# Low parts of 36 weight chunks: negated on ScalarE and completed by an accumulating DMA, in place of a VectorE subtraction

## The chip, the cores and the metric

The kernel runs on one core of a Trainium2 chip. The metric is the device time of one execution in microseconds (us), lower being better. Five engines work side by side, each with its own queue of instructions that it takes in order: TensorE (PE in the profile; PEld is its loading of weights), VectorE (DVE), ScalarE (ACT), GpSimd (POOL) and SyncE (SP). They wait for each other, and for the DMA transfers that they issue, by semaphores.

## The reference

The kernel computes a decoder trunk of two layers, in float32, for 256 tokens of width 2048:

```python
for i in range(DEPTH):                       # DEPTH = 2
    u = rmsnorm(h, mix_pre_g[i])
    if i < N_A:                              # layer 0
        m = short_conv_mixer(u, a_w_in[i], a_conv_w[i], a_w_out[i])
    else:                                    # layer 1
        m = stick_breaking_mixer(u, b_w_q[j], k_sh, v_sh, b_w_o[j])
    h = h + rmsnorm(m, mix_post_g[i])
    u = rmsnorm(h, mlp_pre_g[i])
    h = h + rmsnorm(square(relu(u @ mlp_w_up[i])) @ mlp_w_down[i], mlp_post_g[i])
    if i == N_A - 1:
        k_sh, v_sh = split(rmsnorm(h, kv_norm_g) @ w_kv)
```

`w_in` is 2048 x 6144, the other mixer matrices are 2048 x 2048 or 2048 x 4096, and the MLP's hidden width is 8192.

## The kernel before, in words

**High and low parts.** A matmul takes operands rounded to a shorter format (float32r). To keep the precision, each operand is split into a high part, its rounded value, and a low part, the rest: `hi = round(w)`, `lo = w - hi`. A product is then three matmuls, high by high, high by low and low by high. So every weight that comes in has to be split.

**The stream of weights.** All weights come as one list, `stream`, of 768 chunks of 128 x 1024 float32 (512 KB). `load_one` has SyncE load the next chunk into one of `RAW` = 5 buffers `raw`. `split_one` splits the next chunk: `high_parts` has ScalarE write `hi` (line 173) and `low_part` has VectorE write `lo` (line 184; line 186 where a gain is multiplied in). Both go into rings of `RING` = 7 buffers. After a split the raw buffer is given back and the next load is traced; the load waits until all who read the buffer are done. SyncE takes its loads in order, so those behind a waiting load wait too. `chunk(i)` is called where TensorE uses chunk i, and splits up to `AHEAD` = 4 chunks further.

**Sevens.** Some pairs of chunks, those in the dictionary `sevens`, are used in a scheme with seven products in place of eight. `split_seven` makes four differences of the two raw chunks on VectorE (line 210, the tile `sums`), and splits them and the chunks into four buffers of each ring (named a, b, t and u).

**Input projection.** After a lead, tiles of two chunks and seven pairs alternate. A tile takes the 8 high matmuls of its first chunk, the 8 of its second, and then the low ones in the same order (line 748). The outcome is evicted by `combined` (line 757, the tile `sum`).

**MLP.** The hidden width is cut into `STEPS` = 8 steps. In each of the first seven, two halves (h = 0 and 1) have four up tiles each, and after every up tile one pair of down chunks for the step before (a seven, or an eight). An up tile (`whole_up`) takes two chunks: 16 high matmuls (line 1013), then 16 low ones (line 1020). All these up tiles use one PSUM bank: ScalarE copies half of it (`half`, line 1026), VectorE adds the other half to that (`s`, line 966), and only then can the next up tile begin. Within a step the chunks lie 16 to a half and 4 to an up tile with its pair, so 16h + 4 and 16h + 5 are the chunks of the second up tile of half h, and 16h + 10 and 16h + 11 the pair after the third.

**Accumulating DMAs.** `add_later` evicts four PSUM banks of products to SBUF once in a step (twice in the first), and eight or nine DMAs from GpSimd's queue, issued in `finish` (line 1030), add these 256 KB tiles to the partial results in SBUF (`mg`, by `accum_op=ALU.add`).

**Order.** TensorE's order is that of the program. The other engines' orders come from a planner that runs at build time, with its own estimates of times; within the norms the orders of VectorE and ScalarE are written out by hand.

Of the kernel before, what the change touches and what calls it, by code (L numbers as in the profile page):

```python
# [9 lines left out]
F32 = mybir.dt.float32  # L10
F32R = mybir.dt.float32r
AF = mybir.ActivationFunctionType
ALU = mybir.AluOpType
# [5 lines left out]
KD = D // P  # L19
# [27 lines left out]
STEPS = 8  # L47
# [20 lines left out]
IN_AT = {unit: KD * LEAD // CH + 2 * i for i, unit in enumerate(IN_UNITS)}  # L68
# [27 lines left out]
def trunk(ctx, tc, x, xT, vecs, rows, ws, out):  # L96
    nc = tc.nc
# [45 lines left out]
    raw, parts, early = {}, {}, {}  # L143
    last_load = [None]
    count = {"loaded": 0, "split": 0, "limit": 1 << 30, "apart": False}
    lows = []
    sevens = {}

    def load_one():
        i = count["loaded"]  # L150
        if i >= len(stream):
            return
        w, c = stream[i]
        t = wpool.tile([P, CW], F32, tag="raw", name=f"raw{i}")
        n = HALF if i < FIRST else CW
        for a in range(0, CW, n):
            last_load[0] = nc.sync.dma_start(t[:, a : a + n], w.ap[c, :, a : a + n])
        raw[i] = t
        count["loaded"] += 1

    def pieces_of(i):
        w, c = stream[i]
        gains = w.gains(c) if w.gains else [None] * (4 if i < FIRST else 1)
        n = CW // len(gains)
        return [(slice(j * n, (j + 1) * n), gain) for j, gain in enumerate(gains)]

    def high_parts(i):
        while count["loaded"] <= i:
            load_one()
        hi = wsplit.tile([P, CW], F32R, tag="hi", name=f"whi{i}")  # L170
        lo = wsplit.tile([P, CW], F32R, tag="lo", name=f"wlo{i}")
        for j, (at, gain) in enumerate(pieces_of(i)):
            rounded = nc.scalar.activation(  # L173
                hi[:, at], raw[i][:, at], AF.Copy, scale=1.0 if gain is None else gain
            )
            if j < 2:
                early[i] = rounded
            if not count["apart"]:
                low_part(hi, lo, raw[i], at, gain)
        parts[i] = hi, lo  # L180

    def low_part(hi, lo, t, at, gain):
        if gain is None:
            nc.vector.tensor_tensor(lo[:, at], t[:, at], hi[:, at].bitcast(F32), op=ALU.subtract)  # L184
        else:
            nc.vector.scalar_tensor_tensor(  # L186
                lo[:, at], t[:, at], gain, hi[:, at].bitcast(F32), op0=ALU.mult, op1=ALU.subtract
            )
# [37 lines left out]
    def split_one():  # L226
        i = count["split"]
        if i in sevens:
            split_seven(i)
            return  # L230
        high_parts(i)
        count["split"] += 1
        if count["apart"]:
            lows.append(i)
        else:
            raw.pop(i)
            load_one()
# [138 lines left out]
    h = [None] * NB  # L376
# [310 lines left out]
    W = {"in": Weights(ws["in"]), "out": Weights(ws["out"])}  # L687
# [18 lines left out]
    def convolution(tmp):  # L706
# [71 lines left out]
        scale = {}  # L778
# [104 lines left out]

        for i in range(0, KD, 2):
            sevens[IN_AT["pair", i]] = sevens[IN_AT["pair", i + 1]] = tmp
        new, late, gates = [], {}, {}
        for kind, i in IN_UNITS:
            if kind == "pair":
# [5 lines left out]
            at, n = IN_AT["tile", i], IN_TILES[i]  # L894
# [28 lines left out]
    with tc.tile_pool(name="p_in", bufs=1, reuse_waits="tile") as tmp:  # L923
        y = convolution(tmp)
# [14 lines left out]
    def mlp(pool, i, before, after):  # L939
# [3 lines left out]
        scale = [None] * NB  # L943
# [89 lines left out]
        def lead_up(to):  # L1033
            first = W["mlp", i, 0].base
            place = {kn: m for m, kn in enumerate(UP_FIRST)}
            lead = list(range(LEAD_UP))
            alone = [(k, n) for k in range(ALONE) for n in lead]
            for b in range(NB):
                for k, n in sorted(alone, key=lambda kn: (kn[0] // 4, kn[1] // 3 if kn[0] < 4 else 0)):
                    high(first, place[k, n], k, n, n + 2, b)  # L1040
            for k, n in alone:
                low(first, place[k, n], k, n)
            for k in range(ALONE, KD):
                for n in lead:
                    high(first, place[k, n], k, n, n + 2)
                for n in lead:
                    low(first, place[k, n], k, n)
                    if k == KD - 1:
                        finish(to, n)
            for n in range(LEAD_UP, NF):  # L1050
                whole_up(to, n, first + 2 * n, (n + 2) % 8)
# [114 lines left out]
        for e in range(STEPS):  # L1166
            for h in range(2):
                for m in SEVEN[e][h]:
                    n = 16 * h + 4 * ORDER[h].index(m) + 2 if e < STEPS - 1 else 8 * h + 2 * m
                    sevens[W["mlp", i, e + 1].base + n] = pool  # L1170
        now = Hidden(0)
        lead_up(now)
        for e in range(STEPS):
# [33 lines left out]
    run(project(W["out"], y, 2, sublayer(mix0)), leave=mix0)  # L1207
    kv = KeyNorms(pool0, None)
    mlp(pool0, 0, mix0, kv)


# [181 lines left out]

    pool1, mix1 = held["pool1"], held["mix1"]
    mlp(pool1, 1, mix1, OutNorms(pool1, None))
    pool1.release()

# [79 lines left out]
```

## Time and profile before

| | us |
|---|---|
| runs (three) | 2110.68, 2110.22, 2110.02 |
| median | 2110.22 |
| profiled execution, its own time | 2110.45 |
| its span, first to last instruction | 2108.7 |

| engine | busy us | share |
|---|---|---|
| TensorE | 2090.4 | 99% |
| VectorE | 1835.2 | 87% |
| ScalarE | 1435.2 | 68% |
| GpSimd | 113.7 | 5% |

The granted clock of TensorE was 0.999 of full speed. In the lines shown further on, a group's row has the line, the engine, the operation, the tiles written and read, their shapes, the count, the busy time, the mean of one in ns, and after the second bar the idle time of the engine just before them with what ended it. A wait's row names who waited for what, the total, how often, and the longest. A row of the timeline begins with the start and the length, both in us, and may end with the idle time before it in brackets. The input projection runs from the start to about 270 us, the first MLP from about 365 to 1010 and the second from about 1440 to the end.

### The profile page before, as it was taken

Reading aid. Unit: us, or ns where it says so; the run is one execution under the profiler, and the core shown is the slowest. Engines: PE = TensorE matmul, PEld = TensorE weight load, DVE = VectorE, ACT = ScalarE, POOL = GpSimd, SP = SyncE. Lnnn points to the kernel's source line nnn. Section 1 sums busy time; section 2 is a strip of 40 time slices with the busy share of each in tenths; the row PEclk is TensorE's granted clock in tenths of the full one; section 3 lists DMA queues with packets and bytes.
Section 4 is the critical chain, followed back from the end, with each engine's and each line's share of the span. In section 5 each row is a group of like instructions: output and inputs, shape, how many; then the busy total and the mean of one; then the engine's idle time right before and its main releaser. Section 6 shows DMA issues by size and latency. Waiting matters only on the chain.

```text
span 2108.7 us, 29835 instructions
## 1 busy us (share of the span) xinstructions
PE 2090.4 (99%) x10608; PEld 1782.2 (85%) x10608; DVE 1835.2 (87%) x2807; ACT 1435.2 (68%) x2210; POOL 113.7 (5%) x137
## 2 busy tenths in 40 slices
PE   9999999999999999999999999999999999999998
PEld 8888888888888888888888888889888888888886
DVE  9999965999899999999866777558989999999997
ACT  8656544776776776767567888547767767677674
POOL 0000000010110110101000000000101001011010
PEclk9999999999999999999999999999999999999999
DMA  8467574586777867868575555655778688687683
GB/s 290 155 205 250 191 259 142 190 244 213 232 230 223 265 194 236 250 205 268 173 222 165 160 160 166 218 175 170 199 237 238 213 239 242 210 255 215 220 267 137
DMA packets 132342, 449.23 MB, mean 213 GB/s; under 512 B 14816, under 2 KB 15072, under 8 KB 131168
## 3 DMA queue, kind: packets, MB, share of 16 engines
q1 hardware_dynamic: 113184, 406.55, 58.7%
q0 software_dynamic: 18720, 40.38, 9.9%
q8 instruction: 83, 1.36, 0.3%
q14 instruction: 67, 0.55, 0.1%
q10 hardware_dynamic: 288, 0.39, 0.1%
HBM read 413.19 MB, written 2.10 MB: 197 GB/s over the span
## 4 chain that ended last, share of the span: by engine, by line
PE 91%; DVE 6%; DMA 2%; issue 1%; ACT 1%; DVEq 0%; ACTq 0%
PE up L1013 20%; PE up L1020 11%; PE acc L326 8%; PE acc L328 8%; PE acc L327 8%; PE acc L748 5%; PE more L1121 4%; PE more L1120 4%; PE more L1122 4%; PE acc L1120 4%; PE acc L1121 4%; PE acc L1122 4%; PE lead L748 2%; DVE wlo L184 1%; DMA raw<-w_mlp 1%; PE up L1015 1%
## 5 line engine op out<-in xcount | busy, mean ns | idle before, releaser
L184 DVE TENSOR_TENSOR wlo<-raw,whi 128x1024 fp32r<-128x1024 f32 (+1 forms) x442 | 528.1, 1206 | 87.0 <-ACT whi L173 86.6
L173 ACT ACTIVATE whi<-raw 128x1024 fp32r<-128x1024 f32 (+1 forms) x442 | 453.0, 1043 | 171.1 <-PE acc L328 82.5
L1013 PE MATMUL up<-u,whi 128*128 128x512 f32 x1952 | 465.6, 390 | 3.5 <-DVE s L966 3.5
L1013 PEld LDWEIGHTS up<-u,whi 128*128 128x128 f32 x1952 | 364.6, 188 | 79.9 <-DVE s L966 5.4
L1020 PEld LDWEIGHTS up<-u,wlo 128*128 128x128 f32 x2048 | 263.6, 191 | 10.3
L1020 PE MATMUL up<-u,wlo 128*128 128x256 f32 x2048 | 268.0, 283 | 0.0
L1030 POOL DMA_DIRECT2D mg<-more x108 | 101.7, 1051 | 1280.5 <-ACT s L968 648.3
L186 DVE SCALAR_TENSOR_TENSOR wlo<-raw,gv,whi 128x512 fp32r<-128x512 f32 (+1 forms) x160 | 131.9, 854 | 41.5 <-ACT whi L173 40.8
L210 DVE TENSOR_TENSOR sums<-raw,sums 128x512 f32<-128x512 f32 x236 | 162.1, 687 | 1.3
L173 ACT ACTIVATE whi<-raw,gv 128x512 fp32r<-128x512 f32 (+1 forms) x160 | 121.6, 800 | 48.5 <-PE acc L328 41.8
L326 PE MATMUL acc<-whi,u 128*128 128x512 f32 x384 | 153.1, 399 | 0.1
L328 PE MATMUL acc<-whi,u 128*128 128x512 f32 x384 | 150.0, 391 | 0.0
L327 PE MATMUL acc<-wlo,u 128*128 128x512 f32 x384 | 149.8, 390 | 0.0
L1026 ACT ACTIVATE half<-up 128x256 f32<-128x256 f32 x128 | 48.5, 381 | 89.1 <-PE up L1020 85.5
L748 PE MATMUL acc<-u,whi 128*128 128x512 f32 x416 | 98.9, 391 | 2.7 <-DVE sum L757 2.7
L210 DVE TENSOR_TENSOR sums<-raw,raw 128x512 f32<-128x512 f32 x118 | 81.0, 687 | 23.2 <-DMA raw<-w_mlp 23.0
L967 ACT ACTIVATE s<-s 128x256 f32<-128x256 f32 x128 | 52.4, 413 | 66.3 <-DVE s L966 65.9
L748 PEld LDWEIGHTS acc<-u,whi 128*128 128x128 f32 x416 | 77.4, 188 | 20.5 <-DVE sum L757 3.7
L210 DVE TENSOR_TENSOR sums<-raw 128x512 f32<-128x512 f32 x118 | 81.0, 686 | 11.9 <-DMA raw<-w_mlp 11.7
L328 PEld LDWEIGHTS acc<-whi,u 128*128 128x128 f32 x384 | 72.1, 188 | 15.6
L326 PEld LDWEIGHTS acc<-whi,u 128*128 128x128 f32 x384 | 72.2, 188 | 13.8 <-ACT tk L1309 0.6
L327 PEld LDWEIGHTS acc<-wlo,u 128*128 128x128 f32 x384 | 72.3, 188 | 13.4
(5995 smaller groups left out, 4513.4 us busy)
## 6 DMA issues: line engine op xcount, KB each, us to landing
raw<-w_mlp SPq DMA_DIRECT2D x512, 512.0 KB, 4.6
raw<-w_in SPq DMA_DIRECT2D x94, 512.0 KB, 4.4
mg<-more POOLq DMA_DIRECT2D x108, 256.0 KB, 8.3
raw<-w_out SPq DMA_DIRECT2D x32, 512.0 KB, 4.5
raw<-w_v SPq DMA_DIRECT2D x32, 512.0 KB, 4.3
raw<-w_k SPq DMA_DIRECT2D x32, 512.0 KB, 4.4
raw<-w_q SPq DMA_DIRECT2D x32, 512.0 KB, 4.2
raw<-w_wo SPq DMA_DIRECT2D x32, 512.0 KB, 3.7
```

The costliest lines, as they stand in the source:

```text
L173: rounded = nc.scalar.activation(hi[:, at], raw[i][:, at], AF.Copy, scale=1.0 if gain is None else gain)
L184: nc.vector.tensor_tensor(lo[:, at], t[:, at], hi[:, at].bitcast(F32), op=ALU.subtract)
L210: nc.vector.tensor_tensor(t, x, y, op=ALU.subtract)
L326: nc.tensor.matmul(ps[:], xh, hi[:, a], start=i == 0 and k == 0, stop=False)
L327: nc.tensor.matmul(ps[:], xh, lo[:, a], start=False, stop=False)
L328: nc.tensor.matmul(ps[:], xl, hi[:, a], start=False, stop=i == self.n - 1 and k == self.ks - 1)
L748: nc.tensor.matmul(ps[:, :cols], w, xs[:, :cols], start=k == 0 and part == parts[0], stop=k == KD - 1 and part == parts[1], skip_group_che ...
L1013: nc.tensor.matmul(ps, weight(0, first, m), x, start=k == 0, stop=False)
L1020: nc.tensor.matmul(pss[n][:, :T], weight(1, first, m), x, start=False, stop=k == KD - 1)
L1120: nc.tensor.matmul(self.ps[key][:], xh, hi, start=first, stop=False)
L1121: nc.tensor.matmul(self.ps[key][:], xh, lo, start=False, stop=False)
L1122: nc.tensor.matmul(self.ps[key][:], xl, hi, start=False, stop=last)
```

## The change

For 36 chunks, collected in the set `subtracted`, VectorE's subtraction is left out. ScalarE writes `hi` as before and then, in a second pass over the raw chunk, its negative, rounded in the same way, into the `lo` buffer. A DMA from GpSimd's queue then adds the whole raw chunk (512 KB, from SBUF to SBUF) onto it, which gives `w - hi`. Eight of the 36 are the second chunks of every other tile of the input projection (tiles 5 to 19); 28 are the second chunk of the second up tile of each half, in the first seven steps of both MLPs. The raw buffer of such a chunk is read until the DMA has landed.

```diff
@@ -145,6 +145,7 @@
     sevens = {}
+    subtracted = set()
 
@@ -175,7 +176,10 @@
             if j < 2:
                 early[i] = rounded
-            if not count["apart"]:
+            if i in subtracted:
+                nc.scalar.activation(lo[:, at], raw[i][:, at], AF.Copy, scale=-1.0)
+                nc.gpsimd.dma_start(lo[:, at].bitcast(F32), raw[i][:, at], accum_op=ALU.add)
+            elif not count["apart"]:
                 low_part(hi, lo, raw[i], at, gain)
@@ -883,6 +887,7 @@
             sevens[IN_AT["pair", i]] = sevens[IN_AT["pair", i + 1]] = tmp
+        subtracted.update(IN_AT["tile", i] + 1 for i in range(5, KD + 4, 2))
@@ -1168,6 +1173,8 @@
                     sevens[W["mlp", i, e + 1].base + n] = pool
+                if e < STEPS - 1:
+                    subtracted.add(W["mlp", i, e + 1].base + 16 * h + 5)
```

## The prediction

> **What bounds the kernel now.** I read the page first: busy times and the chain that ended last.
>
> ```profile
> span 2108.7 us, 29835 instructions
> PE 2090.4 (99%) x10608; PEld 1782.2 (85%) x10608; DVE 1835.2 (87%) x2807; ACT 1435.2 (68%) x2210; POOL 113.7 (5%) x137
> ...
> PE 91%; DVE 6%; DMA 2%; issue 1%; ACT 1%; DVEq 0%; ACTq 0%
> ```
>
> TensorE carries 91% of the chain and is busy 2090.4 of 2108.7 us; VectorE, at 87%, is the next engine. So an edit that adds no TensorE work can win only what TensorE loses by waiting, and can lose without such a limit. The waits, over the whole span:
>
> ```profile
> PE acc L748 <- DVE sum L757: 4.7, 5, 1.9
> PE up L1013 <- DVE s L966: 3.5, 4, 1.8
> ...
> DVE sums L210 <- DMA raw<-w_mlp: 34.7, 27, 2.7
> ```
>
> TensorE waits 8.2 us for VectorE in all, in nine places. The third row matters as much: VectorE itself waits 27 times for a weight load in the MLPs. VectorE runs in order, so whatever stands behind such a wait waits too.
>
> Next, four stretches by engine and DMA: the input projection where its eight moved chunks lie, the steady part of the first MLP, a 27 us stretch of it in which GpSimd's accumulating DMAs run (`mg<-more`), and one of 25 us without them.
>
> ```profile
> core 0: us, PE busy (x) PEld busy (x) DVE busy (x) ACT busy (x) POOL busy (x), PEclk, DMA share, GB/s
> 76.00:230.00 154.00, 151.99 (x772) 128.86 (x770) 153.59 (x219) 94.20 (x119) 1.23 (x2) 1.00 0.67 218
> 613.00:1000.00 387.00, 387.00 (x1976) 331.64 (x1976) 366.78 (x531) 275.86 (x416) 40.12 (x46) 1.00 0.79 237
> 613.00:640.00 27.00, 27.00 (x136) 22.98 (x136) 24.84 (x41) 20.29 (x33) 7.92 (x9) 1.00 1.05 279
> 655.00:680.00 25.00, 25.00 (x126) 21.30 (x126) 22.31 (x35) 16.95 (x27) 0.00 (x0) 1.00 0.65 221
> ```
>
> From 613 to 1000 TensorE has no idle time at all: relief of VectorE there is worth nothing. In 613:640 the DMA engines are full (1.05), in 655:680 they are not (0.65). Each MLP step has one such full stretch, early in its second half (h = 1), and one moved chunk of each step (16h + 5 with h = 1) falls into it: 14 of the 36. The other 22 (14 with h = 0, eight in the input projection) meet no `mg<-more`.
>
> **The change, part by part.** Removed is one VectorE subtraction a chunk, added one ScalarE pass.
>
> ```profile
> L184 DVE TENSOR_TENSOR wlo<-raw,whi 128x1024 fp32r<-128x1024 f32 (+1 forms) x442 | 528.1, 1206 | 87.0 <-ACT whi L173 86.6
> L173 ACT ACTIVATE whi<-raw 128x1024 fp32r<-128x1024 f32 (+1 forms) x442 | 453.0, 1043 | 171.1 <-PE acc L328 82.5
> ```
>
> VectorE loses 36 x 1.21 = 43 us of 1835, ScalarE gains 36 x 1.04 = 38 us of 1435. ScalarE is 71% busy in 613:1000 (275.86 of 387), so its pass costs nothing by itself; behind it wait the high part of the next pair and the PSUM eviction `half`, for about 1 us.
>
> Added to GpSimd's queue is one accumulating DMA of 512 KB a chunk. Its price has no row in this trace; the nearest are the 256 KB accumulates and the 512 KB loads, here in 613:640:
>
> ```profile
> q1 hardware_dynamic: 1407, 5.15, 54.3%
> q0 software_dynamic: 1296, 2.36, 50.2%
> ...
> raw<-w_mlp SPq DMA_DIRECT2D x9, 512.0 KB, 6.7
> mg<-more POOLq DMA_DIRECT2D x8, 256.0 KB, 8.6
> ```
>
> GpSimd's nine instructions there (the x9 of the table above) are all accumulates of 256 KB: 50.2% of 27 us, 13.6 us of all 16 engines, 1.5 us each; twice the bytes make 3.0 us. The loads took 54.3%, 14.7 us for 5.15 MB: 1.5 us for one of 512 KB (0.524 MB). So the added transfer takes the engines 1.5 us if it goes like a load, 3.0 us like an accumulate. I take 3.0, the same operation. The Trainium skill (DMA: Bandwidth & Descriptors, "Anatomy of one DMA — SWDGE (gpsimd) path") prices a DMA from GpSimd at about 2.0 us fixed plus its bytes over 436 GB/s, which by its formula is an estimate of 1.2 us of movement for 512 KB; it makes no difference for accumulation, and the row above (1.5 us for 256 KB, where the formula has 0.6) speaks against it. By 1.2 us the sum below would come to +2.9 us instead of +22.5.
>
> *Where there is room.* Over the trace the `mg<-more` landed 3.3 us after issue at the least (row below, with the tightest of the 22 places, the first moved chunk, 27). Alone, the new one should land some 1.5 us later than that, so about 5 us after issue, 6 with loads beside it.
>
> ```profile
> DMA to landing us min/median/max: 3.3/8.3/12.3
> 75.09 1.99 ACT L173 ACTIVATE whi<-raw 128x1024 fp32r<-128x1024 f32 x2
> 77.36 2.35 DVE L184 TENSOR_TENSOR wlo<-raw,whi 128x1024 fp32r<-128x1024 f32 x2
> 84.44 1.83 PE L748 MATMUL acc<-u,wlo 128*128 128x256 f32 x14
> ```
>
> The high part ends at 77.1. Negation 1.0 and DMA 6 give 84.1; the chunk is the second half of its tile, so its low part is needed eight matmuls after 84.44, at 85.4. It fits by 1.3 us. Its raw buffer comes free some 4.5 us later than at 79.7, and with it the load five chunks on; that load has the five-deep ring as cover. I cost these 22 at nothing. If the cover is gone, it is about 1 us a place, up to 20 us. What they can win is in the input projection, where VectorE is busy 153.59 of 154 us:
>
> ```profile
> PE acc L748 <- DVE sum L757: 2.0, 3, 0.9
> ```
>
> That is the waits of 76:230 alone: at most 2.0 us, all of which I take.
>
> *Where there is none.* Around the moved chunk of 613:640 (its high part is made at 618.92), the timelines of GpSimd, ScalarE, VectorE, SyncE and TensorE:
>
> ```profile
> 613.81 0.87 POOL L1030 DMA_DIRECT2D mg<-more  x1 [67.66 <-ACT s L968]
> 617.00 0.87 POOL L1030 DMA_DIRECT2D mg<-more  x1 [2.32 <-ACT more L1082]
> 617.58 1.19 POOL L1030 DMA_DIRECT2D more<-more  x1
> 618.11 2.45 POOL L1030 DMA_DIRECT2D mg<-more  x2
> 621.57 0.87 POOL L1030 DMA_DIRECT2D mg<-more  x1 [1.00 <-DMA mg<-more]
> 626.43 0.87 POOL L1030 DMA_DIRECT2D mg<-more  x1 [3.99 <-DMA mg<-more]
> 618.92 1.06 ACT L173 ACTIVATE whi<-raw 128x1024 fp32r<-128x1024 f32 x1
> 620.39 1.23 DVE L184 TENSOR_TENSOR wlo<-raw,whi 128x1024 fp32r<-128x1024 f32 x1
> 621.64 3.10 SPq L157 DMA_DIRECT2D raw<-w_mlp  x2
> 629.82 0.69 DVE L210 TENSOR_TENSOR sums<-raw 128x512 f32<-128x512 f32 x1
> 632.67 0.69 DVE L210 TENSOR_TENSOR sums<-raw,raw 128x512 f32<-128x512 f32 x1 [2.16 <-DMA raw<-w_mlp]
> 634.41 0.42 DVE L966 TENSOR_TENSOR s<-up,half 128x256 f32<-128x256 f32 x1
> 629.51 2.08 PE L1020 MATMUL up<-u,wlo 128*128 128x256 f32 x16
> 636.21 1.07 PE L1013 MATMUL up<-u,whi 128*128 128x512 f32 x4
> ```
>
> Today the raw buffer is free at 621.6, and SyncE issues the load that waited for it, and 3 us later the next (a `seven` pair needs both). VectorE waits 2.16 us for the second, until 632.67; `s` stands behind that and empties the one PSUM bank of the up tiles at 634.83; TensorE wants it at 636.21. The slack is 1.38 us. After the change the buffer is free only when the accumulate has landed. The negation writes the buffer that VectorE could write from 620.39 on, so it ends near 620.39 + 1.04 = 621.4. By then five accumulates are in the queue, 7.5 us of engine time at 1.5 each; with four of them queued from 617.00 on, some 3 us of that is left. The new one goes behind them: 621.4 + 3 + 3.0, and up to 1.5 us of a load beside it, is 627.4 to 629. The low part is wanted at 630.5, eight matmuls into the row of 629.51, so that just fits. The load is what comes late: it is issued at about 628 instead of 621.6, and SyncE's later loads stand behind it. But the DMA engines are full, so 3.0 us more work ahead of the pair's second load moves its landing by about 3.0 us, and with it the `sums` and `s`. TensorE then stalls for 3.0 less the slack. (The 6 us of later issue don't count in full: a load that starts then meets fewer accumulates.) VectorE's 1.2 us of relief ahead of it only lengthens its wait.
>
> The same reading in all 14 places (slack = next up matmul less the end of `s`) gives, first MLP 0.09, 0.05, 1.38, 2.20, 1.50, 2.80, 1.02, second 0.46, 0.05, 1.12, 2.20, 0.89, 2.78, 1.00 us. First and last of the 14:
>
> ```profile
> 466.91 0.42 DVE L966 TENSOR_TENSOR s<-up,half 128x256 f32<-128x256 f32 x1
> 467.42 0.93 PE L1013 MATMUL up<-u,whi 128*128 128x512 f32 x3
> ...
> 2035.19 0.42 DVE L966 TENSOR_TENSOR s<-up,half 128x256 f32<-128x256 f32 x1
> 2036.61 1.07 PE L1013 MATMUL up<-u,whi 128*128 128x512 f32 x4
> ```
>
> The sum of (3.0 less slack), none below nothing, is 24.5 us. With the 2.0 us won: +22.5. The profiled execution took 2110.45 us (1.75 outside its span), 0.23 above the median of 2110.22, so the sums are made from 2110.45: **2133 us**. With 2.0 us of delay (the engines are not quite full at each instant) the 14 give 12.4 and the total is 2121; with 4.0, 38.5 and 2147.
>
> **The rivals.**
>
> *VectorE's relief wins (faster).* Mechanism: the planner orders VectorE anew, and where it puts `s` ahead of the two `sums`, the load's delay is off TensorE's path. It decides at one point: `s` before `sums<-raw,raw` in the 14 places. Then the 2.0 us of the projection and the 3.5 us of `up <- DVE s` go: 2110.45 - 5.5 = 2105 us. For it: VectorE is busy all the time in the projection and 95% of 613:1000, so it is late often. Against: in 613:640 the planner put `sums` first although it had to wait. Chance 0.27, most of it beyond 0.2%.
>
> *The accumulate queues behind more.* If its place in GpSimd's order is behind the add of 621.57, 1.5 us more stand ahead of it: 4.5 us of delay, 14 x 4.5 - 17.5 = 45.5, total 2153 us. Behind the add of 626.43, which itself waits 3.99 us for a landing, it is some 6.5 us: +71.5, 2182 us, and the low part too comes after 630.5. For it: GpSimd is in order and these adds are ready early. Against: by the estimate above the negation ends just before 621.57. Chance 0.18.
>
> *The transfer is cheaper or covered.* At a load's 1.5 us the 14 places cost 7.4, total 2116 us; with a cover I don't see, nothing, and 2108. Middle 2112. The share of 1.05 speaks against it. Chance 0.10. The Trainium skill's formula (DMA: Bandwidth & Descriptors, the section above) would end here, at 2113; no row of this trace goes by it.
>
> **How the numbers follow.** Forecast 0.45, queue 0.18, relief 0.27, cheaper 0.10. About 0.2% (4.2 us) is what a measurement of this kernel can tell from no change. Faster by more: 0.23, from the relief. Within: 0.11, the rest of the relief and most of "cheaper". Slower by more: 0.66. Range: the forecast alone is 2121 to 2147; with the relief's 2105 and the nearer queue case, 2104 to 2153 us. Left out are the second queue case and a relief above all waits I can see.
>
> **What would show it.** Right: the VectorE row of the low parts counts 406 instead of 442; the wait `sums <- DMA raw<-w_mlp` grows from 34.7 us by 20 to 40; `up L1013 <- DVE s` grows from 3.5 to about 25, in the h = 1 stretches; 655:680 and its like stay without waits. Wrong: TensorE waits for the new DMA itself at L1020 (queue rival); `s` stands ahead of `sums` and `up <- s` falls (relief); new accumulates land within 4 us in the full stretches (cheaper); waits appear in the 22 quiet places, which I costed at nothing.

## The result, and the profile after

The changed kernel takes 2232.4 us (median; 2230.7 to 2234.0), the kernel before 2110.1 beside it: a ratio of 1.058 (95% interval 1.0562 to 1.0599). It is slower by 122 us, where 22.5 were forecast. First the page of the changed kernel, with the rows that answer to those shown of before.

```profile
span 2229.3 us, 29885 instructions
PE 2123.6 (95%) x10608; PEld 1808.9 (81%) x10608; DVE 1806.3 (81%) x2771; ACT 1474.9 (66%) x2246; POOL 144.3 (6%) x173
...
PE 65%; DMA 14%; DVE 9%; issue 6%; ACT 4%; POOL 1%; POOLq 0%; DVEq 0%; ACTq 0%; SPq 0%
...
L188 DVE TENSOR_TENSOR wlo<-raw,whi 128x1024 fp32r<-128x1024 f32 (+1 forms) x406 | 485.9, 1205 | 106.1 <-ACT whi L174 91.5
```

VectorE's row of low parts lost 42 us (528.1 to 485.9) and ScalarE gained 40, as worked out; all of VectorE's busy time fell by 29 only, and what took the rest back is not shown. TensorE fell from 91% of the chain to 65%, and DMAs rose from 2% to 14%. The 120.6 us that the span grew can be split by TensorE's own row: its idle time grew from 18.3 to 105.7 us (+87.4), and its busy time from 2090.4 to 2123.6 (+33.2) with the same 10608 matmuls. TensorE's waits in the changed kernel, and who waited for loads on VectorE:

```profile
PE up L1025 <- DMA wlo<-raw: 86.5, 15, 8.5
PE acc L752 <- DMA wlo<-raw: 4.2, 3, 2.0
PE acc L752 <- DVE sum L761: 2.7, 2, 2.0
...
DVE sums L214 <- DMA raw<-w_mlp: 61.8, 40, 2.9
```

Nearly all of the new idle time is one wait: at the low matmuls of the up tile (L1025, L1020 before), for the landing of the accumulating DMA. Of the 15, 14 are the h = 1 places, 4.5 to 8.5 us each and 85.7 together. The wait of the up tiles for `s`, on which the forecast rested, is gone altogether. The place that the prediction worked through, in the changed kernel:

```profile
646.20 1.06 ACT L180 ACTIVATE wlo<-raw 128x1024 fp32r<-128x1024 f32 x1
639.62 0.86 POOL L1035 DMA_DIRECT2D mg<-more  x1 [34.33 <-ACT s L973]
642.81 0.86 POOL L1035 DMA_DIRECT2D mg<-more  x1 [2.33 <-ACT more L1087]
643.39 1.17 POOL L1035 DMA_DIRECT2D more<-more  x1
643.93 2.41 POOL L1035 DMA_DIRECT2D mg<-more  x2
647.15 0.86 POOL L1035 DMA_DIRECT2D mg<-more  x1 [0.81 <-DMA mg<-more]
650.99 0.86 POOL L1035 DMA_DIRECT2D mg<-more  x1 [2.98 <-DMA mg<-more]
651.53 1.21 POOL L181 DMA_DIRECT2D wlo<-raw  x1
657.40 0.69 DVE L214 TENSOR_TENSOR sums<-raw 128x512 f32<-128x512 f32 x1 [2.78 <-DMA raw<-w_mlp]
659.93 0.69 DVE L214 TENSOR_TENSOR sums<-raw,raw 128x512 f32<-128x512 f32 x1 [1.84 <-DMA raw<-w_mlp]
664.95 0.43 DVE L971 TENSOR_TENSOR s<-up,half 128x256 f32<-128x256 f32 x1 [1.99 <-ACT half L1031]
654.63 1.11 PE L1025 MATMUL up<-u,wlo 128*128 128x256 f32 x8
662.42 2.07 PE L1025 MATMUL up<-u,wlo 128*128 128x256 f32 x8 [6.68 <-DMA wlo<-raw]
669.68 3.79 PE L1018 MATMUL up<-u,whi 128*128 128x512 f32 x16
```

The negation is done at 647.3. Seven adds stand ahead in GpSimd's queue, and the seventh waits 2.98 us for an earlier one's landing, so the chunk's DMA goes out at 651.53, 4.3 us after its data is ready, and lands at 662.4, 10.85 us after its issue. TensorE's first eight low matmuls end at 655.7; the other eight wait 6.68 us. It is so in all 14 places: seven adds ahead, 3.6 to 5.8 us from the end of the negation to the issue (61.6 together), and 7.9 to 11.4 us from there to the landing. VectorE's `sums` wait for the pair's two loads, 2.78 and 1.84 us, more than before, but nobody pays for it: TensorE is late itself, `s` stands ready in time, and the matmuls at 669.68 wait for nothing.

The same place by stretches, with the granted clock (PEclk, third column from the end):

```profile
core 0: us, PE busy (x) PEld busy (x) DVE busy (x) ACT busy (x) POOL busy (x), PEclk, DMA share, GB/s
649.00:655.00 6.00, 6.00 (x30) 5.03 (x29) 5.62 (x8) 4.35 (x6) 2.43 (x3) 1.00 1.09 278
655.00:662.40 7.40, 0.74 (x7) 0.54 (x5) 3.16 (x5) 0.63 (x1) 1.04 (x2) 0.75 1.05 227
662.40:665.50 3.10, 3.08 (x11) 2.87 (x12) 1.11 (x3) 0.38 (x1) 0.00 (x0) 0.50 0.71 212
665.50:668.00 2.50, 2.50 (x12) 2.01 (x11) 1.63 (x2) 2.22 (x3) 0.00 (x0) 1.00 1.03 408
```

When the work comes back at 662.4, TensorE runs at half clock for 3.1 us and so loses about 1.5. The trace's record of the clock has half clock at the end of each of the 14 waits or just behind it, over 3.1 to 6.1 us of the work that follows, 63.1 in all, and once more near 276 us: 66.5 us of work, half of which, 33.3, is the 33.2 us of additional busy time (31.5 of it in the 14 places). The Trainium skill (TensorE: Matmul & The Clock Gate, "Part 1: The HAM clock gate (the "warmup" mystery)") has the array fall to half clock after an idle window of about 3.4 us and come back after about as long of work; this trace agrees in the place shown (0.50 for 3.1 us after a wait of 6.68 us). It does not everywhere: from 276.4 to 279.8 us the clock is at 0.50 after a wait of only 1.99 us, and there the measurement decides.

### The profile page after: what moved, and what is told of

The parts are those of the page before. It is cut to its first block, busy times and chain, and to the rows that moved or that the text cites. A ratio compares the mean times of both kernels' runs of the same rounds, so it can differ in the third digit from the quotient of the medians.

```text
span 2229.3 us, 29885 instructions
## 1 busy us (share of the span) xinstructions
PE 2123.6 (95%) x10608; PEld 1808.9 (81%) x10608; DVE 1806.3 (81%) x2771; ACT 1474.9 (66%) x2246; POOL 144.3 (6%) x173
## 3 DMA queue, kind: packets, MB, share of 16 engines
q0 software_dynamic: 23904, 59.26, 13.8%
## 4 chain that ended last, share of the span: by engine, by line
PE 65%; DMA 14%; DVE 9%; issue 6%; ACT 4%; POOL 1%; POOLq 0%; DVEq 0%; ACTq 0%; SPq 0%
PE up L1018 11%; DMA wlo<-raw 8%; PE up L1025 7%; PE acc L330 7%; PE acc L332 7%; PE acc L331 7%; PE acc L1125 3%; PE acc L1126 3%; PE acc L1127 3%; PE more L1125 3%; PE more L1126 3%; PE more L1127 3%; DVE wlo L188 2%; DMA mg<-more 2%; PE acc L752 2%
## 5 line engine op out<-in xcount | busy, mean ns | idle before, releaser
L188 DVE TENSOR_TENSOR wlo<-raw,whi 128x1024 fp32r<-128x1024 f32 (+1 forms) x406 | 485.9, 1205 | 106.1 <-ACT whi L174 91.5
L1025 PE MATMUL up<-u,wlo 128*128 128x256 f32 x2048 | 283.8, 291 | 86.5 <-DMA wlo<-raw 86.5
L1025 PEld LDWEIGHTS up<-u,wlo 128*128 128x128 f32 x2048 | 274.9, 198 | 100.0 <-DMA wlo<-raw 89.7
L181 POOL DMA_DIRECT2D wlo<-raw x36 | 35.6, 989 | 948.6 <-ACT half L1031 487.3
L971 DVE TENSOR_TENSOR s<-up,half 128x256 f32<-128x256 f32 x128 | 53.5, 419 | 41.9 <-ACT half L1031 41.5
```

The costliest lines, as they stand in the source:

```text
L1025: nc.tensor.matmul(pss[n][:, :T], weight(1, first, m), x, start=False, stop=k == KD - 1)
```

## The experiments

Two theories were left after this. *Queue*: GpSimd's order puts the DMA of an h = 1 chunk behind seven adds, TensorE waits for its landing, and half clock follows. *Held buffer*, the forecast's step: the raw buffer is given back late, and a load, VectorE's `sums` and `s` are late with it. A third was that every moved chunk costs alike.

### Only the 22 chunks that meet no adds

```diff
-                if e < STEPS - 1:
+                if e < STEPS - 1 and h == 0:
                     subtracted.add(W["mlp", i, e + 1].base + 16 * h + 5)
```

> 22 moved chunks: the eight of the input projection and the 14 with h = 0; the 14 with h = 1 go back to VectorE. Queue theory (GpSimd's order puts the new DMA of an h = 1 chunk behind seven adds, TensorE waits 4.5 to 8.5 us for the low part and then runs some us at half clock): nearly all of the 122 us goes, 2112 to 2118 us; what stays are the four short waits of 0.8 to 2.0 us seen in the quiet places (5 us), less up to 2 us won. Rival, every moved chunk costs the same (122/36 = 3.4 us): 2185 us. Rival, full DMA engines delay the loads (the forecast's step): 2108 to 2112 us.

Measured 2117.1 us beside 2109.5, ratio 1.0032 (1.0018 to 1.0045).

```profile
PE up L1018 <- DVE s L971: 3.7, 4, 1.5
PE acc L752 <- DMA wlo<-raw: 3.3, 2, 2.2
```

So these 22 cost 7.6 us (3.8 to 9.5 by the interval), and not the 75 of the third theory. But they don't win 2.0 either.

### Only the 14 chunks that meet them

```diff
-        subtracted.update(IN_AT["tile", i] + 1 for i in range(5, KD + 4, 2))
...
-                if e < STEPS - 1:
+                if e < STEPS - 1 and h == 1:
                     subtracted.add(W["mlp", i, e + 1].base + 16 * h + 5)
```

> Only the 14 chunks with h = 1 are moved. Queue theory: 14 x (6.1 us of wait + about 2 us of half clock) = 113 us, 2215 to 2230 us, and more where the planner now puts all nine adds ahead (up to 2250). Same cost for every chunk: 2158 us. Loads delayed by full engines, as forecast: about 2135 us.

Measured 2226.7 us, ratio 1.0545 (1.0525 to 1.0566).

```profile
PE up L1024 <- DMA wlo<-raw: 86.9, 14, 9.6
```

14 waits in 14 places: these chunks carry 117 of the 122 us, and with the 7.6 of the 22 it adds up within the intervals.

### The eight chunks of the input projection alone

```diff
-                if e < STEPS - 1:
-                    subtracted.add(W["mlp", i, e + 1].base + 16 * h + 5)
```

> Only the eight chunks of the input projection are moved. The prediction booked 2.0 us won here (waits of acc on sum that go) and nothing lost: 2108 us. From the run with 22 chunks moved, which still waits 3.3 us for two landings (second and fifth of the eight): +1 to +6 us, 2111 to 2116. Same cost for every chunk (3.4 us): 2137.

Measured 2113.3 us beside 2110.6, ratio 1.0016 (1.0007 to 1.0025). 2.7 us are lost where 2.0 were booked as won, so some 5 of the 7.6 us above should lie in the MLPs; this is an estimate, a difference of two runs whose intervals are about 2 us or more each way.

### The chunk's DMA ahead of the adds

```diff
-                nc.gpsimd.dma_start(lo[:, at].bitcast(F32), raw[i][:, at], accum_op=ALU.add)
+                added[0] = nc.gpsimd.dma_start(lo[:, at].bitcast(F32), raw[i][:, at], accum_op=ALU.add)
...
-                with tc.issue_after(copied.ins):
+                with tc.issue_after(added[0].ins):
                     nc.gpsimd.dma_start(a, more, accum_op=ALU.add)
```

> All 36 moved, but GpSimd issues a step's adds only after the moved chunk's DMA of that half. Queue theory: the DMA goes out about 0.3 us after the negation and lands 5 to 8 us later, as in the quiet places; the 14 waits fall from 86 us to under 15 in all, total 2112 to 2130 us. Theory of full engines: the same bytes move in the same stretch, the loads are late all the same, 2133 us or more, with the wait on s at the up tiles. Same cost for every chunk: 2232 us.

Measured 2173.8 us, ratio 1.0301 (1.0279 to 1.0324). This was outside what the queue theory allowed. The page's row of engines, TensorE's waits, and the place again:

```profile
PE 2108.3 (97%) x10608; PEld 1790.2 (83%) x10608; DVE 1798.7 (83%) x2771; ACT 1462.0 (67%) x2246; POOL 144.3 (7%) x173
```

```profile
PE up L1019 <- DVE s L972: 39.1, 17, 6.3
PE up L1026 <- DMA wlo<-raw: 3.7, 5, 1.9
```

```profile
628.24 0.86 POOL L182 DMA_DIRECT2D wlo<-raw  x1 [42.22 <-DVE sums L215]
633.66 0.33 SPq L159 DMA_DIRECT2D raw<-w_mlp  x1
643.58 0.69 DVE L215 TENSOR_TENSOR sums<-raw,raw 128x512 f32<-128x512 f32 x1 [5.03 <-DMA raw<-w_mlp]
646.53 0.42 DVE L972 TENSOR_TENSOR s<-up,half 128x256 f32<-128x256 f32 x1
647.00 6.65 PE L1019 MATMUL up<-u,whi 128*128 128x512 f32 x16 [6.30 <-DVE s L972]
```

The wait for the low part is gone (86.5 to 3.7 us), as the queue theory says. In its place stands the forecast's: SyncE stands 2.8 us for the landing of the DMA of 628.24 and issues the pair's second load at 633.66; the load takes 9.9 us beside the adds that now come after; VectorE waits 5.03 us for it, `s` stands behind, and TensorE waits 6.30 us. Both theories hold, one behind the other. How much of the load's delay is the held buffer and how much the adds, which this edit moved behind the DMA, no run separates. But SyncE's rows point to the buffer: in eight of the 14 places the load that waits for the DMA is the pair's second, in the other six it is the one after the pair, and the eight have 31.6 of the 39.1 us.

### Nobody on TensorE waits for the DMA

```diff
-            if i in subtracted:
-                nc.scalar.activation(lo[:, at], raw[i][:, at], AF.Copy, scale=-1.0)
-                nc.gpsimd.dma_start(lo[:, at].bitcast(F32), raw[i][:, at], accum_op=ALU.add)
-            elif not count["apart"]:
+            if not count["apart"]:
                 low_part(hi, lo, raw[i], at, gain)
+            if i in subtracted:
+                nc.gpsimd.dma_start(raw[i][:, at], raw[i][:, at], accum_op=ALU.add)
```

> VectorE makes all low parts as before; at the same 36 places GpSimd still issues a 512 KB accumulating DMA behind the same adds, from the raw buffer onto itself, which nobody reads. So the raw buffer is held, the later loads wait and the DMA engines carry the bytes, but TensorE never waits for a landing. Forecast's step (a held buffer and full engines delay the loads, VectorE's sums and s): +24 us for the delay of 3.0 us, more since the hold is longer, 2135 to 2165 us. Queue theory in its pure form (only the wait for the low part costs): 2110 to 2116 us.

Measured 2209.0 us, ratio 1.0468 (1.0449 to 1.0487): +99 us with no low part late, more than either theory gave. TensorE's largest wait, then the place:

```profile
PE up L1017 <- DVE s L970: 58.8, 19, 6.6
```

```profile
641.32 0.85 POOL L1034 DMA_DIRECT2D mg<-more  x1 [3.17 <-issue]
642.16 0.89 POOL L182 DMA_DIRECT2D raw<-raw  x1
654.30 0.69 DVE L213 TENSOR_TENSOR sums<-raw,raw 128x512 f32<-128x512 f32 x1 [7.00 <-DMA raw<-w_mlp]
656.04 0.42 DVE L970 TENSOR_TENSOR s<-up,half 128x256 f32<-128x256 f32 x1
656.52 5.75 PE L1017 MATMUL up<-u,whi 128*128 128x512 f32 x16 [5.65 <-DVE s L970]
```

Here the DMA goes out behind the seventh add and lands at 650.25; only then does SyncE issue the load that needs the buffer, and VectorE, which makes all low parts again, waits 7.00 us for it. Holding a buffer of the raw ring until a DMA that stands behind others has landed costs 99 us here, against the 122 of the kernel in which TensorE waits for the outcome.

### Useless work ahead of the wait

```diff
         def whole_up(to, n, first, number):
+            if first + 1 in subtracted and n == 5:
+                pss[n] = bank(number, "up")
+                for _ in range(16):
+                    x = u[0][:, 0].rearrange("p a b t -> p (a b t)")
+                    nc.tensor.matmul(pss[n][:], weight(0, first, 0), x, start=True, stop=True)
```

> The changed kernel, with 16 useless matmuls (128x512, 0.227 us each, 3.6 us) put on TensorE at the start of each of the 14 up tiles whose low part comes late; their outcome is overwritten. They end before the wait. If the wait is for a landing that does not depend on TensorE, it shortens by 3.6 us a place and the work costs nothing; if besides TensorE runs at half clock after a long wait, that goes too: in all 10 to 30 us less than the 2232 of the changed kernel, 2200 to 2222, and the granted clock rises from 0.978 to 0.99 or more. If the clock is no part of it: 2232. If the late landing moves along with TensorE's own pace: 14 x 3.6 = 51 us more, 2283.

Measured 2215.5 us, ratio 1.0492 (1.0478 to 1.0507): 17 us faster than the changed kernel, with 224 matmuls more.

```profile
PE 2155.8 (98%) x10832; PEld 1835.5 (83%) x10832; DVE 1807.2 (82%) x2771; ACT 1475.0 (67%) x2246; POOL 144.0 (7%) x173
```

```profile
PE up L1025 <- DMA wlo<-raw: 35.6, 14, 4.7
```

The wait fell by 51 us, which is the time of the useless matmuls (224 x 0.227). Without them TensorE is busy 2155.8 - 50.8 = 2105.0 us instead of 2123.6: 18.6 us of the half clock went with the shorter waits (by the record of the clock, work at half clock fell from 66.5 to 27.5 us). So the landing does not depend on TensorE's pace, and the clock is a cost of its own.

### The forecast's own assumption: five adds ahead

```diff
             for a, more in adds[:3]:
-                with tc.issue_after(copied.ins):
+                behind["n"] += 1
+                with tc.issue_after(copied.ins if behind["n"] <= 5 else added[0].ins):
```

(`behind["n"]` begins at 0 with each `add_later`; `added` as above.)

> The situation that the forecast assumed: all 36 moved, five adds may go ahead of the h = 1 chunk's DMA, the others come after it. Forecast's price (delay of the pair's load 3.0 us less the slack): 2133 us. Between the runs so far (none ahead 2174, seven ahead 2232), if the number of adds ahead is what counts through the landing: 2180 to 2215, with both waits, L1025 for the low part and the up tile for s.

Measured 2190.4 us, ratio 1.0379 (1.0361 to 1.0397).

```profile
PE 2117.2 (97%) x10608; PEld 1797.9 (82%) x10608; DVE 1799.5 (82%) x2771; ACT 1467.4 (67%) x2246; POOL 144.1 (7%) x173
```

```profile
PE up L1020 <- DVE s L973: 29.7, 10, 5.1
PE up L1027 <- DMA wlo<-raw: 21.9, 12, 4.1
```

The DMA now goes out 0.29 us after the negation in all 14 places, so the queue holds it nowhere; it lands 8.6 to 10.8 us after its issue, and in 12 of the 14 TensorE waits for it. The waits for `s` come from the held buffer: 28.5 of the 29.7 us lie in the eight places where the pair's second load waits for the DMA. With none, five and seven ahead: 2174, 2190 and 2232 us.

### The pair's work behind `s`

```diff
-            split_seven(i)
+            if i in behind_s:
+                with tc.issue_after(latest["s"].ins), tc.issue_after(latest["half"].ins):
+                    split_seven(i)
+            else:
+                split_seven(i)
```

(On top of the kernel with the DMA ahead of the adds. `behind_s` has the pairs 16h + 10 with h = 1, `latest` the last `s` and `half` that were traced.)

> None ahead (as e4_first), and VectorE's and ScalarE's work on the pair that waits for the late load (16h + 10, h = 1) is put behind s and half of the up tile before. If the 60 us of e4_first come through s standing behind sums that wait for a load: the wait up <- s (39 us) goes nearly all, and half clock with it, 2115 to 2135 us, with some waits left where the pair itself is late. If they come from the load being late for the pair itself: 2165 to 2180, the wait only moves to the pair's matmuls.

Measured 2142.6 us, ratio 1.0148 (1.0134 to 1.0161), 31 us less than without this order but over what was expected.

```profile
PE 2101.6 (98%) x10608; PEld 1781.1 (83%) x10608; DVE 1797.8 (84%) x2771; ACT 1455.8 (68%) x2246; POOL 144.7 (7%) x173
```

```profile
PE up L1024 <- DVE s L977: 15.8, 16, 2.4
```

So about half of the 64 us that the kernel with none ahead loses came through `s` standing behind `sums`. The other half stays: `s` is still late by about 1 us in 16 places, and TensorE is busy 11 us longer than before although the granted clock is 0.998 again. In the place shown for that kernel the load is as late as it was: `sums` wait 5.12 us for it, TensorE then waits 1.64 us for the pair's own low part, and VectorE, busy without a break, comes to the next `s` 0.91 us late. What the rest is stays open.

### The kernel before, with that order alone

The same order on the kernel before: no chunk moved, no adds put behind a DMA.

> The kernel before with that order alone (pair behind s and half, h = 1), nothing moved. If the waits up <- DVE s of the kernel before (3.5 us) come from the same order: 2106 to 2109 us, a little faster than before. If the order makes the pair late: 2110 to 2120.

Measured 2108.2 us beside 2110.7, ratio 0.9988 (0.9979 to 0.9996).

```profile
PE up L1018 <- DVE s L971: 0.5, 1, 0.5
```

The wait fell from 3.5 to 0.5 us, and the time by about 2.5. It is the one version here that beats the kernel before by more than its interval, and narrowly.

### That order, and five quiet chunks moved

```diff
+        subtracted.update(IN_AT["tile", i] + 1 for i in (9, 11, 15, 17, 19))
```

(With the order of the last run, and no chunk of the MLPs moved.)

> The order of e9_before_order, and the five chunks of the input projection that showed no wait (tiles 9, 11, 15, 17, 19) moved. If VectorE's relief of 5 x 1.2 us is worth anything where it is busy all the time: up to 2 us below e9_before_order, 2106 to 2108 us. If the planner's new order or late loads take it back: 2108 to 2113.

Measured 2111.3 us, ratio 1.0004 (0.9995 to 1.0013): nothing won that can be told from no change, and what the order had given is not seen any more.

## Why the prediction was wrong

**The step that failed** first is the place in GpSimd's queue. "The new one goes behind them", the five adds in the queue at 621.4, assumed that a DMA takes its place when its data is ready. The planner had fixed the order at build time: in all 14 places seven adds come first, and in the place shown the seventh waits for a landing. So TensorE waits for the DMA itself (85.7 us in the 14 places) and not for `s`. The rival of the queue named this, down to the add that waits 3.99 us, at 0.18; its argument against, that the negation is ready before 621.57, was an argument about readiness and not about order. Its price, 2182, was still 50 us short.

The queue is not the whole miss. With five ahead, as the forecast assumed, the kernel takes 2190 us: 42 less than the changed one, but 57 above the forecast of 2133 and outside its range. Three more terms were wrong.

**The low part "just fits"**: 629 at the latest against 630.5. In the place shown, 15.1 us pass from the end of the negation to the landing where 6.0 to 7.6 were booked: 4.3 in the queue, 10.85 from issue to landing. Even with five ahead it does not fit; TensorE waits 21.9 us there. The sum had the engines' time for the bytes and nothing for the way from issue to landing, although its own row shows such a time: 3.3 us at the least for an add whose bytes take 1.5. Those 1.8 us would have made it 629.2 to 630.8, an estimate from these rows. What the loads beside the DMA add to that stays open.

**The held buffer** is a mechanism that exists, and with five ahead its size is near its price (29.7 us of waits for `s`, 24.5 booked). That is partly luck: the prediction had it in all 14 places, and here it lies in ten, nearly all of it in eight. In the changed kernel it costs TensorE nothing: `up <- s` fell to nothing, although the `sums` waits grew from 34.7 to 61.8 us, by the 20 to 40 that were to show the forecast right. Which load the buffer holds back decides. Before, the load that came for the chunk's buffer was the first of the next pair's. In the changed kernel that pair's two loads go out at 649.73 and 650.83, before the DMA itself, and the load that waits for it is the one after them, issued at 662.40; it is so in all 14 places. Where it is the pair's second (eight of the 14 with none and with five ahead), `s` comes late.

**Half clock** was in no term of the sum. In the changed kernel it is 33 of 121 us, and with five ahead 23 of 79 (46.4 us of work at half clock).

**The quiet 22 at nothing, with 2.0 won**: they lose 7.6. The first of the eight, for which 1.3 us of room was found, was to land 6 us after issue; it took 7.1, and TensorE waits 0.77 us. The landings of all 36 moved chunks took 5.0 us at the least and 7.8 in the median; of these 22, 5.0 to 9.7.

```profile
DMA to landing us min/median/max: 5.0/7.8/11.4
```

**Right** were TensorE as the bound without which nothing is won, the count of 406 on VectorE, and the price of the transfer. In all, GpSimd's queue took, before and after:

```profile
q0 software_dynamic: 18720, 40.38, 9.9%
```

```profile
q0 software_dynamic: 23904, 59.26, 13.8%
```

That is 9.9% of 2108.7 = 208.8 us and 13.8% of 2229.3 = 307.6, so 98.9 / 36 = 2.7 us a chunk, near the 3.0 taken from the accumulates and far from a load's 1.5 and from the 1.2 estimated by the Trainium skill's formula (DMA: Bandwidth & Descriptors, "Anatomy of one DMA — SWDGE (gpsimd) path"), with which this trace does not agree for accumulating DMAs.

The relief of VectorE, 0.27 as a rival, shows no gain even where it could be had without a wait: the five quiet chunks won nothing. What it could have won by way of the order, that order gives without it (2108.2 us).

## What to carry to other kernels

A DMA put on a queue takes the place that the queue's order gives it, not the one that its data's readiness suggests: list what stands ahead in that order, and ask of each whether it waits. Price the DMA from issue to landing, and not by its bytes alone. Count the buffer that the DMA reads as well as the one it writes, and see which load takes that buffer next: in these runs the delay went to whoever stood behind that load. On an engine that is busy 99%, price a wait of several microseconds with the time at half clock that follows it.

## What was not expected of the hardware

TensorE's clock: after waits of 4.5 to 8.5 us it runs at half clock for 3.1 to 6.1 us of work (0.50 in 662.4:665.5), and 224 matmuls whose outcome is thrown away made the kernel 17 us faster, since they shorten the waits. And accumulating 512 KB within SBUF takes the 16 DMA engines 2.7 us, nearly twice what a load of 512 KB from HBM takes (1.5 us in the stretch of the prediction).
